# Down projection: the lo part of u and the left sums kept in HBM for the second half of the columns, and seven products for every second pair of k-tiles there

## The chip, the cores and the metric

The kernel runs on one core of one Trainium2 chip. The metric is device time in microseconds (us), from single executions on the chip; lower is better. The engines are TensorE (PE in the profile, PEld for its weight loads), VectorE (DVE), ScalarE (ACT), GpSimd (POOL) and SyncE (SP). SP and POOL issue nearly all transfers here.

## The reference

One decoder layer over 256 positions with a width of 2048: two attentions over one input projection, an output projection, and then the MLP, which alone matters here:

```python
h = _rmsnorm(x, norm_mlp_pre[layer])
u = jnp.square(jax.nn.relu(h @ w_up[layer]))        # (256, 8192)
x = x + _rmsnorm(u @ w_down[layer], norm_mlp_post[layer])
```

All of it is float32. `w_down` is 8192 x 2048, so the down projection contracts over 64 k-tiles of 128 rows.

## The kernel before

**Split operands.** TensorE multiplies in the form fp32r, so each float32 operand x is split into two tiles, hi and lo: ACT writes hi as a rounded copy, and DVE writes lo = x - hi (`split`, L288 to L292). A product of two operands takes three matmuls of 128x128 by 128x512: hi with hi, hi with lo, lo with hi (`three`).

**Weights.** `Weights` is one stream of weight tiles for the whole kernel. A plain tile is loaded by SP into one of five `raw` buffers (L173) and then split into one of eight pairs of `hi` and `lo` buffers. `plan` puts a tile into the stream; `emit` writes its load and split some tiles ahead of the product that needs it. A function listed in `weights.first[i]` is called just before tile i is emitted. Each engine runs its instructions in the order in which they were emitted, so this order is also the order on DVE, ACT, POOL and SP.

**Down projection.** It runs in two halves of 1024 columns (c = 0, then c = 1), each over 32 pairs of k-tiles. `uT[g]` holds u transposed, four k-tiles for each of the 16 groups g; `split_u` makes its hi and lo (`uhi`, `ulo`, two buffers each) one group ahead, in each half anew.

A plain pair costs 2 tiles x 4 output blocks x 3 = 24 matmuls. The pairs in `DOWN_SEVEN` go by Strassen's scheme in Winograd's form instead, with seven block products, 7 x 3 = 21 matmuls. This text calls such a pair a *seven*. It needs work that a plain pair does not:

- its two weight tiles are loaded by POOL into `ab_down`, which has one buffer (`load_two`, L357);
- `sums` in `seven` forms t and u from them in `st_down` with three DVE adds (L343, L347, L348);
- four tiles are split from these: the corner b11 (128x512) and b from `ab_down`, u and t from `st_down`. The next load of the first half of `ab_down` has to wait for the split of b11, and that of the second half for the split of b;
- `down_sums` (`four_sums`, L910 to L912) and `down_split` form the left sums from u and split them into `shi` and `slo`.

`plan_seven` chooses where `sums` with its load is emitted:

```python
at = max(len(weights.specs) - SUMS_AHEAD, after)     # SUMS_AHEAD = 2; after = end of the seven before
for n, f in (*more, (0, sums)):
    weights.first.setdefault(at - n, []).append(f)
```

So `sums` comes two weight tiles before the seven's first tile, but not before the last tile of the seven ahead of it. Half c = 0 has its sevens at pairs 7, 10, 13, ..., 28 (8 of them), half c = 1 at 3, 6, 9, ..., 27 (9 of them). A plain pair has two weight tiles, so two plain pairs, four tiles, lie between two sevens.

**Other work on DVE in the down projection.** `close` combines the extra products (`md`) at the end of each half; `half_evac` adds them to the first half's results and scales these (L1099 to L1103), early in the second half; `x_back` brings the residual x back from HBM late in the second half.

Of the kernel before, what the change touches and what calls it, by code (L numbers as in the profile page):

```python
# [26 lines left out]
P = 128  # L27
# [18 lines left out]
CW = 1024  # L46
# [51 lines left out]
for _i, _n in enumerate(((11, 12), (13,), (14, 15))):  # L98
    UP_STEPS += [("w", _i)] + [("k", k) for k in _n]

DOWN_SEVEN = (range(7, 29, 3), range(3, 28, 3))
GT = FF // 512
DOWN_STEPS = [[s for kp in range(2 * GT)
               for s in ([("w", kp)] if kp in ws else [("k", 2 * kp), ("k", 2 * kp + 1)])] for ws in DOWN_SEVEN]

# [143 lines left out]
def layer(nc, tc, io):  # L249
# [9 lines left out]
    dram = tc.alloc_tile_pool(name="dram", bufs=1, space=bass.MemoryType.DRAM)  # L259
# [28 lines left out]
    def split(hi, lo, src, g=None):  # L288
        if g is not None:
            return split_gain(hi, lo, src, g)  # L290
        nc.scalar.activation(hi, src, AF.Copy)  # L291
        nc.vector.tensor_tensor(out=lo, in0=src, in1=hi.bitcast(F32), op=OP.subtract)  # L292
# [6 lines left out]
    def tok(t, k, b):  # L299
        return t[:, k, b * P:(b + 1) * P]  # L300
# [25 lines left out]
    def up_weight(j, k):  # L326
        return io["w_up"][k * P:(k + 1) * P, j * CW:(j + 1) * CW]

    late = {}
# [36 lines left out]

        return seven(load, lambda: [late["up"].tile([P, CW], F32, tag="T", bufs=2, name=f"{n}{j}_{kp}") for n in "tu"])

    def plan_seven(sums, fs, after, more=()):

        at = max(len(weights.specs) - SUMS_AHEAD, after)
        for n, f in (*more, (0, sums)):
            weights.first.setdefault(at - n, []).append(f)
        return [weights.plan(f) for f in fs], len(weights.specs)

# [15 lines left out]
    def seven_down(c, kp):  # L391
        def load():
            return load_two(dpl["ab"], nc.gpsimd, io["w_down"][2 * kp * P:(2 * kp + 2) * P, c * CW:(c + 1) * CW])

        return seven(load, lambda: [late["st"][:, i * CW:(i + 1) * CW] for i in range(2)])

    dpl, left, wide_d = {}, {}, []
    for c in range(2):
        wide_d.append([])
        for what, k in DOWN_STEPS[c]:  # L400
            if what == "k":
                ts = [weights.plan(down_weight(c, k), 1, CW)]
            else:
                q, parts_q = (lambda c=c, k=k: down_sums(c, k)), (lambda c=c, k=k: down_split(c, k))
                ts, after = plan_seven(*seven_down(c, k), after, ((2, q), (1, parts_q)))
            wide_d[c].append((what, k, ts))

    def in_order(n, apart=(0, 0)):
# [335 lines left out]
    for what, ch in ch_b:  # L744
# [8 lines left out]
        else:  # L753
# [4 lines left out]
            after = [kr_chain, k_chain[pr]] + ([pair_chain[pr - 1]] if pr else [])  # L758
# [87 lines left out]
    for ns in ((0, 1), (2,), (3,)):  # L846
# [4 lines left out]
        for c, b, acc in proj(mixT, [ch_o[n] for n in ns], f"o{ns[0]}", order, heads_done):  # L851
            n = ns[c]
            if not late:
# [8 lines left out]
                                  in_=io["norm_attn_post"].partition_broadcast(P).rearrange("p o d -> p (o d)"))  # L862
# [11 lines left out]
    uT = {}  # L874
# [22 lines left out]
    def split_u(c, g):  # L897
        if (c, g) == (0, 0):
            uh, ul = [wp.tile([P, CW], F32R, tag=w, bufs=W_BUFS, name=f"u{w}0").rearrange("p (k s) -> p k s", k=4)
                      for w in ("hi", "lo")]  # L900
        else:
            uh, ul = [dpl["dp"].tile([P, 4, S], F32R, tag=f"u{w}", bufs=2, name=f"u{w}{c}_{g}") for w in ("hi", "lo")]
        split(uh.rearrange("p k s -> p (k s)"), ul.rearrange("p k s -> p (k s)"), uT[g].rearrange("p k s -> p (k s)"))
        return uh, ul

    def four_sums(q, f):

        tt = nc.vector.tensor_tensor
        fs, qs = [x.rearrange("p (k s) -> p k s", s=P) for x in (f, q)]
        tt(out=qs[:, 0:2], in0=fs[:, 0:2], in1=fs[:, 1:4:2], op=OP.subtract)  # L910
        tt(out=qs[:, 2], in0=qs[:, 0], in1=fs[:, 3], op=OP.add)
        tt(out=qs[:, 3], in0=fs[:, 2], in1=qs[:, 2], op=OP.subtract)  # L912

    def down_sums(c, kp):
        q = late["st"][:, 2 * CW:2 * CW + 512]
        k = 2 * (kp % 2)
        four_sums(q, uT[kp // 2][:, k:k + 2, :].rearrange("p k s -> p (k s)"))
        left[c, kp] = q

    def down_split(c, kp):  # L920
        st = [dpl["dp"].tile([P, 512], F32R, tag=f"s{w}", bufs=2, name=f"s{w}{c}_{kp}") for w in ("hi", "lo")]
        split(*st, left[c, kp])
        left[c, kp] = [[t[:, i * P:(i + 1) * P] for t in st] for i in range(4)]

    sums = []

# [44 lines left out]
    def close(c, m):  # L971

        tt = nc.vector.tensor_tensor
        nc.scalar.activation(c[0], m[1], AF.Copy)
        for out, x, y, op in ((1, m[6], c[0], OP.subtract), (2, m[7], c[1], OP.subtract),
                              (1, m[5], c[1], OP.add), (3, c[1], m[7], OP.subtract)):
            tt(out=c[out], in0=x, in1=y, op=op)
# [7 lines left out]
    for j in range(FF // CW):  # L985
# [9 lines left out]
        for t, b in order:  # L995
            what, k, tiles = steps[t]
# [26 lines left out]
            first, last = k == 0, k == N_SEVEN - 1  # L1023
# [4 lines left out]
            if last:  # L1028
                more = close(closing(j), m)
# [87 lines left out]
    us = {(0, 0): u_next}  # L1117
    for c in range(2):

        for i, (b, n) in enumerate(PARTS):  # L1120
            y[b][2 * c + n] = bank(4 * c + i, f"y{b}{2 * c + n}")
        accs = {(b, n): y[b][2 * c + n] for b, n in PARTS}
        ws = DOWN_SEVEN[c]
        for t, (what, k, tiles) in enumerate(wide_d[c]):
            g = (2 * k if what == "w" else k) // 4
            u = us[c, g]
            if g >= GT - 2 and c:
                break
            if what == "k":
                w = weights.get(tiles[0])  # L1130
                for b, n in PARTS:
                    down_mm(c, u, k, b, n, w, t == 0, t == len(wide_d[c]) - 1)
                    flow.pump()
                weights.free(tiles[0])
            else:
                if k == ws[0]:
                    if not c:
                        flow.finish(*u_last)
                    else:
                        flow.finish(h_evac)  # L1140
                    m = {i: bank(4 * (1 - c) + o, f"md{i}_{c}") for o, i in enumerate((1, 6, 7, 5))}
                blocks = [[tok(u[x], 2 * (k % 2) + kk, bb) for x in range(2)] for kk, bb in ((0, 0), (1, 0), (1, 1))]
                seven_products(tiles, (blocks, left.pop((c, k))), accs, m, k == ws[0], k == ws[-1])
                if k == ws[-1]:
                    more = close([spare(10, i) for i in range(4)] if c else closing("d"), m)
            nxt = (c, g + 1) if g < GT - 1 else (1, 0)
            if nxt not in us:
                us[nxt] = split_u(*nxt)
            if (c, what, k) == (0, "k", 3):
                weights.limit += 1  # L1150
            if (c, what, k) == (0, "k", 36):
                g_half = [late["up"].tile([P, 512], F32, tag="r", bufs=2, name=f"g_half{n}") for n in range(2)]
                for n in range(2):
# [5 lines left out]
        if not c:  # L1159
            h_evac = flow.start(half_evac(more, g_half))  # L1160
# [64 lines left out]
```

## Time and profile before

| | us |
|---|---|
| median of 3 runs (1053.62 to 1054.93) | 1054.91 |
| the profiled execution | 1055.26 |
| its span, from the first to the last instruction | 1053.5 |
| PE busy, 4863 matmuls | 1042.6 |
| DVE busy | 819.8 |
| ACT busy | 622.5 |
| POOL busy | 46.7 |
| groups `y` and `md` (down projection) in the chain that ended last | 27% and 4% of the span |

The granted TensorE clock was 0.997 of full speed over the span. The profile's page gives busy times and, in 40 slices, the busy share of each engine in tenths. Its chain is followed back from the last instruction. The view of waits says which engine waited for whom; the timeline gives single instructions with their start and length; windows give the busy time in a stretch. A wait of an engine off the chain costs nothing by itself. Line numbers are those of the kernel before; in the changed kernel the same lines stand a few further down (L292 is L294, L343 is L345, L357 is L359).

### The profile page before, as it was taken

The page shows a single profiled execution, that of the slowest core. Times are in us where ns is not written, and L with a number is a line of the kernel's source. Part 1 is how long each engine was busy: PE and PEld are TensorE (multiplying, and loading weights), DVE is VectorE, ACT ScalarE, POOL GpSimd, SP SyncE. Part 2 cuts the span into 40 slices and gives each one's busy share as a digit, 9 for nine tenths or more (in the row PEclk, how much of TensorE's full clock was granted, in tenths as well). Part 3 has the DMA queues.
Part 4 walks back from the last instruction along what each step waited for, and adds up shares of the span by engine and source line. Part 5 has one row for each costly group of instructions (what it writes and reads, how often), then busy time and mean ns, then how long its engine had stood idle before and what let it go on. Part 6 is the DMA issues. An engine that isn't in the chain of part 4 may idle for free.

```text
span 1053.5 us, 13402 instructions
## 1 busy us (share of the span) xinstructions
PE 1042.6 (99%) x4863; PEld 869.2 (83%) x4863; DVE 819.8 (78%) x1090; ACT 622.5 (59%) x832; POOL 46.7 (4%) x88
## 2 busy tenths in 40 slices
PE   9999999999999999999999999999999999999996
PEld 6888889888888788888888888888888888888885
DVE  6676536567557679879888888887899988998985
ACT  6584536565545467666665666666566665666661
POOL 0000000000000000010000100000000000000000
PEclk9999999999999999999999999999999999999998
DMA  9975447454447295647656466467466564667732
GB/s 299 355 236 145 144 130 241 143 161 158 141 167 234 79 350 167 222 143 237 197 186 201 160 215 207 148 224 238 162 218 206 195 221 148 224 210 253 262 121 80
DMA packets 74306, 206.26 MB, mean 196 GB/s; under 512 B 6912, under 2 KB 11520, under 8 KB 73856
## 3 DMA queue, kind: packets, MB, share of 16 engines
q1 hardware_dynamic: 63584, 168.06, 49.0%
q0 software_dynamic: 10080, 36.70, 9.7%
q8 instruction: 38, 0.62, 0.2%
q10 hardware_dynamic: 576, 0.64, 0.2%
q14 instruction: 28, 0.23, 0.1%
HBM read 201.18 MB, written 4.19 MB: 195 GB/s over the span
## 4 chain that ended last, share of the span: by engine, by line
PE 97%; DVE 1%; issue 1%; DMA 0%; ACT 0%; POOL 0%; DVEq 0%; POOLq 0%; ACTq 0%
PE y L281 27%; PE acc_u L281 25%; PE acc_o L281 8%; PE m L281 5%; PE md L281 4%; PE acc_qk L281 4%; PE acc_v L281 4%; PE acc_ckv L281 2%; PE acc_ukv L281 2%; PE acc_q L281 2%; PE acc_cq L281 2%; PE acc_k L281 2%; PE acc_uq L281 2%; PE rt L285 1%; PE sc_b L281 1%
## 5 line engine op out<-in xcount | busy, mean ns | idle before, releaser
L292 DVE TENSOR_TENSOR lo<-raw,hi 128x1024 fp32r<-128x1024 f32 (+3 forms) x219 | 249.2, 1153 | 93.8 <-ACT hi L291 93.1
L291 ACT ACTIVATE hi<-raw 128x1024 fp32r<-128x1024 f32 (+3 forms) x219 | 215.9, 1001 | 117.1 <-PE y L281 40.0
L281 PE MATMUL y<-hi,uhi 128*128 128x512 f32 x394 | 153.6, 390 | 0.0
L281 PE MATMUL y<-hi,ulo 128*128 128x512 f32 x394 | 153.3, 389 | 0.0
L281 PE MATMUL y<-lo,uhi 128*128 128x512 f32 x394 | 153.3, 389 | 0.0
L281 PE MATMUL acc_u<-hi,hT_hi 128*128 128x512 f32 x386 | 153.2, 397 | 0.0
L281 PE MATMUL acc_u<-hi,hT_lo 128*128 128x512 f32 x386 | 150.9, 391 | 0.4 <-DVE hT_lo L292 0.4
L281 PE MATMUL acc_u<-lo,hT_hi 128*128 128x512 f32 x386 | 150.6, 390 | 0.0
L296 DVE SCALAR_TENSOR_TENSOR lo<-raw,gcol,hi 128x1024 fp32r<-128x1024 f32 x86 | 107.6, 1278 | 12.5 <-ACT hi L295 12.3
L295 ACT ACTIVATE hi<-raw,gcol 128x1024 fp32r<-128x1024 f32 x86 | 97.9, 1151 | 24.2 <-PE acc_u L281 13.6
L281 PEld LDWEIGHTS y<-hi,uhi 128*128 128x128 f32 x394 | 74.0, 188 | 15.3
L281 PEld LDWEIGHTS y<-lo,uhi 128*128 128x128 f32 x394 | 74.0, 188 | 15.3
L281 PEld LDWEIGHTS y<-hi,ulo 128*128 128x128 f32 x394 | 73.9, 188 | 15.3
L281 PEld LDWEIGHTS acc_u<-hi,hT_lo 128*128 128x128 f32 x386 | 72.4, 188 | 16.2 <-DVE hT_lo L292 0.8
L281 PEld LDWEIGHTS acc_u<-lo,hT_hi 128*128 128x128 f32 x386 | 72.6, 188 | 14.2
L281 PEld LDWEIGHTS acc_u<-hi,hT_hi 128*128 128x128 f32 x386 | 72.6, 188 | 14.0
L281 PE MATMUL acc_o<-hi,mixT_hi 128*128 128x512 f32 x128 | 51.8, 405 | 0.0
L281 PE MATMUL acc_o<-hi,mixT_lo 128*128 128x512 f32 x128 | 50.2, 392 | 0.0
L281 PE MATMUL acc_o<-lo,mixT_hi 128*128 128x512 f32 x128 | 50.0, 390 | 0.0
L291 ACT ACTIVATE hi<-ab 128x512 fp32r<-128x512 f32 (+1 forms) x38 | 32.0, 843 | 30.0 <-PE acc_u L281 23.2
L281 PE MATMUL m<-hi,st 128*128 128x512 f32 x126 | 45.6, 389 | 0.0
L292 DVE TENSOR_TENSOR lo<-st_down,hi 128x1024 fp32r<-128x1024 f32 x34 | 40.9, 1218 | 2.7 <-ACT hi L291 2.7
(309 smaller groups left out, 1947.7 us busy)
## 6 DMA issues: line engine op xcount, KB each, us to landing
raw<-in_w_down SPq DMA_DIRECT2D x94, 512.0 KB, 4.7
raw<-in_w_up SPq DMA_DIRECT2D x86, 512.0 KB, 4.5
raw<-in_w_in SPq DMA_DIRECT2D x55, 512.0 KB, 5.0
ab<-in_w_up POOLq DMA_DIRECT2D x36, 512.0 KB, 4.9
ab_down<-in_w_down POOLq DMA_DIRECT2D x34, 512.0 KB, 6.2
raw<-in_w_out SPq DMA_DIRECT2D x32, 512.0 KB, 4.0
raw<-in_w_in SPq DMA_DIRECT2D x16, 288.0 KB, 2.8
raw<-in_w_ukv SPq DMA_DIRECT2D x8, 512.0 KB, 4.8
```

The lines of the kernel that those rows point to most:

```text
L281: nc.tensor.matmul(out, a, b, start=start, stop=stop)
L285: nc.tensor.transpose(out, a, ident)
L291: nc.scalar.activation(hi, src, AF.Copy)
L292: nc.vector.tensor_tensor(out=lo, in0=src, in1=hi.bitcast(F32), op=OP.subtract)
L295: nc.scalar.activation(hi, src, AF.Copy, scale=g)
L296: nc.vector.scalar_tensor_tensor(out=lo, in0=src, scalar=g, in1=hi.bitcast(F32), op0=OP.mult, op1=OP.subtract)
```

## The change

**Which pairs are sevens.** `DOWN_SEVEN` becomes pairs 7, 11, 13, 17, 19, 23, 25, 29 in the first half (8, as before) and 3, 5, 7, ..., 27 in the second (13 in place of 9). In the second half one plain pair, two weight tiles, lies between two sevens; in the first half distances of two and four pairs alternate.

**What is kept.** The lo part of u of groups 1 to 15 is written to HBM in the first half (`keep_u`, 15 stores of 512 KB on SP) and loaded back in the second (15 loads on POOL) in place of the DVE subtraction; ACT still makes the hi part. The split left sums of the seven pairs that are sevens in both halves (`SHARED`: 7, 11, 13, 17, 19, 23, 25) are stored by `keep_s` (7 stores on SP) and loaded by `down_back` (7 loads on POOL), in place of `four_sums` and their split. The hi and lo of the left sums become one tile, `s`.

The core of the diff:

```diff
-DOWN_SEVEN = (range(7, 29, 3), range(3, 28, 3))
+DOWN_SEVEN = ((7, 11, 13, 17, 19, 23, 25, 29), range(3, 28, 2))
+SHARED = [k for k in DOWN_SEVEN[0] if k in DOWN_SEVEN[1]]
...
+    def down_parts(c, kp):
+        st = dpl["dp"].tile([P, CW], F32R, tag="s", bufs=2, name=f"s{c}_{kp}")
+        return st, [[st[:, w * 512 + i * P:w * 512 + (i + 1) * P] for w in range(2)] for i in range(4)]
...
+    def down_back(c, kp):
+        st, left[c, kp] = down_parts(c, kp)
+        nc.gpsimd.dma_start(out=st.bitcast(F32), in_=skeep[kp])
...
-    def plan_seven(sums, fs, after, more=()):
+    def plan_seven(sums, fs, after, more=(), last=()):
         at = max(len(weights.specs) - SUMS_AHEAD, after)
-        for n, f in (*more, (0, sums)):
+        for n, f in (*more, (0, sums), *((0, f) for f in last)):
             weights.first.setdefault(at - n, []).append(f)
...
+                more = ((), (back,)) if c and k in SHARED else (((2, q), (1, parts_q)),)
+                ts, after = plan_seven(*seven_down(c, k), after, *more)
...
+        u, h, l = [x.rearrange("p k s -> p (k s)") for x in (uT[g], uh, ul)]
+        if c and g:
+            nc.scalar.activation(h, u, AF.Copy)
+            nc.gpsimd.dma_start(out=l.bitcast(F32), in_=ukeep[g])
+        else:
+            split(h, l, u)
...
+    def keep_u(g):
+        ukeep[g] = dram.tile([P, CW], F32, name=f"ukeep{g}")
+        nc.sync.dma_start(out=ukeep[g], in_=us[0, g][1].rearrange("p k s -> p (k s)").bitcast(F32))
+
+    def keep_s(kp):
+        st, skeep[kp] = skeep[kp], dram.tile([P, CW], F32, name=f"skeep{kp}")
+        nc.sync.dma_start(out=skeep[kp], in_=st.bitcast(F32))
...
+                if not c and k in SHARED:
+                    keep_s(k)
             nxt = (c, g + 1) if g < GT - 1 else (1, 0)
             if nxt not in us:
+                if not c and g > 1:
+                    keep_u(g - 1)
                 us[nxt] = split_u(*nxt)
```

**How the order on DVE moves.** Before, in the second half, from the split of b of the seven at pair 9 to the first add for the seven at pair 12 (`raw` rows are plain weight tiles, `uT` rows the left sums and the lo part of u, brackets the semaphores waited for):

```order
L292 TENSOR_TENSOR lo_7955<-ab_down,hi_7954 128x1024 [waits Activation_49]
L292 TENSOR_TENSOR ulo_4_7965<-uT_4464,uhi_4_7964 128x1024 [waits Activation_49]
L292 TENSOR_TENSOR lo_7969<-st_down,hi_7968 128x1024 [waits Activation_49]
L292 TENSOR_TENSOR lo_7985<-st_down,hi_7984 128x1024 [waits Activation_49]
L910 TENSOR_TENSOR st_down<-uT_4831 128x256
L911 TENSOR_TENSOR st_down<-st_down,uT_4831 128x128 [waits DVE_49]
L912 TENSOR_TENSOR st_down<-uT_4831,st_down 128x128 [waits DVE_49]
L292 TENSOR_TENSOR lo_8006<-raw_8003,hi_8005 128x1024 [waits DMAHW2_49,Activation_49]
L292 TENSOR_TENSOR ulo_5_8022<-uT_4485,uhi_5_8021 128x1024 [waits PE_49,Activation_49]
L292 TENSOR_TENSOR slo_12_8026<-st_down,shi_12_8025 128x512 [waits Activation_49]
L292 TENSOR_TENSOR lo_8032<-raw_8029,hi_8031 128x1024 [waits DMAHW3_49,Activation_49]
L343 TENSOR_TENSOR st_down<-ab_down 128x1024 [waits DMASW3_49,DMASW2_49]
```

Twelve rows lie in this stretch: after the split of b come two splits from `st_down`, the work on u and two plain tiles, and the add that reads `ab_down` is last. In the changed kernel, from the first plain tile ahead of the seven at pair 9 to the plain tiles behind it:

```order
L294 TENSOR_TENSOR lo_7967<-raw_7964,hi_7966 128x1024 [waits DMAHW4_49,Activation_49]
L294 TENSOR_TENSOR lo_7989<-raw_7986,hi_7988 128x1024 [waits DMAHW5_49,Activation_49]
L294 TENSOR_TENSOR lo_8005<-ab_down,hi_8004 128x512 [waits Activation_49]
L294 TENSOR_TENSOR lo_8012<-ab_down,hi_8011 128x1024 [waits Activation_49]
L294 TENSOR_TENSOR lo_8022<-st_down,hi_8021 128x1024 [waits Activation_49]
L294 TENSOR_TENSOR lo_8032<-st_down,hi_8031 128x1024 [waits Activation_49]
L345 TENSOR_TENSOR st_down<-ab_down 128x1024 [waits DMASW2_49,DMASW1_49,DVE_49]
L349 TENSOR_TENSOR st_down<-st_down,ab_down 128x512 [waits DVE_49]
L350 TENSOR_TENSOR st_down<-st_down,ab_down 128x512 [waits DVE_49]
L294 TENSOR_TENSOR lo_8051<-raw_8048,hi_8050 128x1024 [waits DMAHW6_49,Activation_49]
```

The add that reads the next `ab_down` now stands right behind the last split of the seven before it, ahead of the two plain tiles, and the rows on u are gone (pair 11 is one of the seven shared ones).

**How the order on POOL moves.** Before, in the second half, POOL issued only the loads of `ab_down`:

```order
L357 DMA ab_down<-in_w_down 128x1024 [waits DMASW4_49,DVE_49]
L357 DMA ab_down<-in_w_down 128x1024 [waits DMASW5_49,DVE_49]
L357 DMA ab_down<-in_w_down 128x1024 [waits DMASW6_49,DVE_49]
L357 DMA ab_down<-in_w_down 128x1024 [waits DMASW7_49,DVE_49]
L357 DMA ab_down<-in_w_down 128x1024 [waits DMASW0_49,DVE_49]
```

In the changed kernel, from the loads for the seven at pair 7 to those for the seven at pair 11:

```order
L359 DMA ab_down<-in_w_down 128x1024 [waits DMASW7_49,DVE_49]
L359 DMA ab_down<-in_w_down 128x1024 [waits DMASW0_49,DVE_49]
L389 DMA s_7_7874<-skeep_6640 128x1024 [waits DMAHW1_49,PE_49]
L929 DMA ulo_3_7895<-ukeep_6658 128x1024 [waits DMASW6_49]
L359 DMA ab_down<-in_w_down 128x1024 [waits DMASW2_49,DVE_49]
L359 DMA ab_down<-in_w_down 128x1024 [waits DMASW3_49,DVE_49]
L929 DMA ulo_4_7983<-ukeep_6741 128x1024 [waits DMASW1_49,PE_49]
L359 DMA ab_down<-in_w_down 128x1024 [waits DMASW6_49,DVE_49]
L359 DMA ab_down<-in_w_down 128x1024 [waits DMASW7_49,DVE_49]
```

The loads of the kept left sums (`s`) and of the lo part of u (`ulo`) stand between the loads of `ab_down`; those that wait for PE wait until it has read the buffer's former contents.

More of the change, by code (lines that the diff above doesn't have):

```diff
@@ L367, in seven_up, with down_sums, down_split @@
         return seven(load, lambda: [late["up"].tile([P, CW], F32, tag="T", bufs=2, name=f"{n}{j}_{kp}") for n in "tu"])
-    def plan_seven(sums, fs, after, more=()):
+    def down_sums(c, kp):
+        q = late["st"][:, 2 * CW:2 * CW + 512]
+        k = 2 * (kp % 2)
+        four_sums(q, uT[kp // 2][:, k:k + 2, :].rearrange("p k s -> p (k s)"))
+        left[c, kp] = q
+    def down_parts(c, kp):
+        st = dpl["dp"].tile([P, CW], F32R, tag="s", bufs=2, name=f"s{c}_{kp}")
+        return st, [[st[:, w * 512 + i * P:w * 512 + (i + 1) * P] for w in range(2)] for i in range(4)]
+    def down_split(c, kp):
+        q = left[c, kp]
+        st, left[c, kp] = down_parts(c, kp)
+        split(st[:, :512], st[:, 512:], q)
+        skeep[kp] = st
+    def down_back(c, kp):
+        st, left[c, kp] = down_parts(c, kp)
+        nc.gpsimd.dma_start(out=st.bitcast(F32), in_=skeep[kp])
+    def plan_seven(sums, fs, after, more=(), last=()):
         at = max(len(weights.specs) - SUMS_AHEAD, after)
-        for n, f in (*more, (0, sums)):
+        for n, f in (*more, (0, sums), *((0, f) for f in last)):
             weights.first.setdefault(at - n, []).append(f)
@@ L395, in seven_down @@
         return seven(load, lambda: [late["st"][:, i * CW:(i + 1) * CW] for i in range(2)])
-    dpl, left, wide_d = {}, {}, []
+    dpl, left, skeep, wide_d = {}, {}, {}, []
     for c in range(2):
@@ L403, in layer @@
             else:
-                q, parts_q = (lambda c=c, k=k: down_sums(c, k)), (lambda c=c, k=k: down_split(c, k))
-                ts, after = plan_seven(*seven_down(c, k), after, ((2, q), (1, parts_q)))
+                q, parts_q, back = [lambda c=c, k=k, f=f: f(c, k) for f in (down_sums, down_split, down_back)]
+                more = ((), (back,)) if c and k in SHARED else (((2, q), (1, parts_q)),)
+                ts, after = plan_seven(*seven_down(c, k), after, *more)
             wide_d[c].append((what, k, ts))
@@ L902, in split_u @@
             uh, ul = [dpl["dp"].tile([P, 4, S], F32R, tag=f"u{w}", bufs=2, name=f"u{w}{c}_{g}") for w in ("hi", "lo")]
-        split(uh.rearrange("p k s -> p (k s)"), ul.rearrange("p k s -> p (k s)"), uT[g].rearrange("p k s -> p (k s)"))
-        return uh, ul
+        u, h, l = [x.rearrange("p k s -> p (k s)") for x in (uT[g], uh, ul)]
[4 more added lines that the diff above has]
+            split(h, l, u)
+        return uh, ul
+    def keep_u(g):
[4 more added lines that the diff above has]
+        nc.sync.dma_start(out=skeep[kp], in_=st.bitcast(F32))
     def four_sums(q, f):
@@ L912, in four_sums @@
         tt(out=qs[:, 3], in0=fs[:, 2], in1=qs[:, 2], op=OP.subtract)
[L914 to L923, printed above, removed]
     sums = []
@@ L1115, in layer @@
     dpl["ab"] = dp.tile([P, 2 * CW], F32, name="ab_down")
-    us = {(0, 0): u_next}
+    us, ukeep = {(0, 0): u_next}, {}
     for c in range(2):
@@ L1159, in layer @@
         if not c:
+            keep_u(GT - 1)
             h_evac = flow.start(half_evac(more, g_half))
```

## The prediction

> **What bounds the kernel now.** I read the busy times first, then TensorE's own waits, then the windows and the chain in the down projection.
>
> ```profile
> PE 1042.6 (99%) x4863; PEld 869.2 (83%) x4863; DVE 819.8 (78%) x1090; ACT 622.5 (59%) x832; POOL 46.7 (4%) x88
> ```
>
> ```profile
> PE warm L476 <- DVE zero L473: 1.2, 1, 1.2
> PE acc_qk L281 <- ACT hi L291: 0.7, 1, 0.7
> PE acc_u L281 <- DVE hT_lo L292: 0.4, 1, 0.4
> PE qrt L285 <- DVE qT L715: 0.2, 1, 0.2
> ```
>
> These four are all of TensorE's waits (us in total, times, longest): 2.5 us, none in the down projection. The kernel is bound by the count of its matmuls. The windows show how near the next engine is, in the second half of the columns:
>
> ```profile
> 720.00:860.00 140.00, 140.00 (x619) 115.91 (x618) 122.34 (x136) 85.89 (x93) 8.64 (x16) 1.00 0.59 200
> 898.00:960.00 62.00, 62.00 (x275) 51.36 (x274) 61.22 (x72) 38.93 (x43) 4.32 (x8) 1.00 0.64 213
> ```
>
> After the length come PE, PEld, DVE, ACT and POOL busy, then the granted clock, the DMA share and GB/s. In the first half (720 to 860) DVE is busy 87% of the time, early in the second 99%, with TensorE still at 100% and the clock at 1.00. The chain gives the pace:
>
> ```profile
> 898.14 10.88 PE y L281 x48
> ...
> 913.78 10.88 PE y L281 x48
> ```
>
> 48 matmuls take 10.88 us, 0.2267 us each. A plain pair (24) is 5.44 us and a seven (21) 4.76 us; two plain pairs and a seven are the 15.64 us from 898.14 to 913.78. After the change one plain pair and one seven repeat: 10.2 us.
>
> **Matmuls removed.** The second half has four more sevens, the first half as many as before: 4 x 3 = 12 matmuls fewer, 12 x 0.2267 = 2.7 us off the path, if TensorE stays the bound.
>
> **The loop through the one buffer ab_down.** These rows show one load from its release to its use (POOL, then DVE):
>
> ```profile
> 903.24 0.54 POOL L357 DMA_DIRECT2D ab_down<-in_w_down  x1 [0.59 <-DVE lo L292]
> ```
>
> ```profile
> 901.12 1.82 DVE L292 TENSOR_TENSOR lo<-ab_down,hi 128x512 fp32r<-128x512 f32 x2
> ...
> 906.27 0.41 DVE L910 TENSOR_TENSOR st_down<-uT 128x256 f32<-128x256 f32 x1
> ...
> 907.26 1.22 DVE L292 TENSOR_TENSOR lo<-raw,hi 128x1024 fp32r<-128x1024 f32 x1
> 908.39 0.68 DVE L292 TENSOR_TENSOR slo<-st_down,shi 128x512 fp32r<-128x512 f32 x1
> 908.99 1.22 DVE L292 TENSOR_TENSOR lo<-raw,hi 128x1024 fp32r<-128x1024 f32 x1
> 910.13 1.22 DVE L343 TENSOR_TENSOR st_down<-ab_down 128x1024 f32<-128x1024 f32 x1
> ...
> 912.72 2.35 DVE L292 TENSOR_TENSOR lo<-raw,hi 128x1024 fp32r<-128x1024 f32 x2
> 914.99 1.82 DVE L292 TENSOR_TENSOR lo<-ab_down,hi 128x512 fp32r<-128x512 f32 x2
> ```
>
> ```profile
> DMA ab_down<-in_w_down: 4.0, 2
> DMA to landing us min/median/max: 4.0/6.2/9.2
> ```
>
> The split of b ends at 902.94 (901.12 + 1.82). POOL issues the second half of the next load 0.3 us later; landing takes a median of 6.2 us from issue. The add waits for it only twice, 4.0 us in all, because 7.2 us of other splits stand between (902.94 to 910.13). In the changed order only u and t stand there (two splits, 1.14 us apart by 907.26 to 908.39: 2.3 us; pairs that aren't shared also have the left sums, 1.0 us by 906.27 to 907.26, and their split, 0.6 by 908.39 to 908.99). The two plain tiles come behind the add. So every seven runs through a closed loop: split of b ends, 0.3 to issue, 6.2 to landing, 0.1 to start, then from the add to the end of the next split of b 910.13 to 916.81, 6.7. That is 13.3 us, against 10.2 us that TensorE takes: 3.1 us short for each seven, whatever else DVE is spared. The left sums lie within the wait.
>
> The same placement exists in the up projection between its second and third seven, and DVE does wait there:
>
> ```profile
> 506.15 1.23 DVE L292 TENSOR_TENSOR lo<-ab,hi 128x1024 fp32r<-128x1024 f32 x1 [1.33 <-ACT hi L291]
> ...
> 511.46 1.22 DVE L343 TENSOR_TENSOR t<-ab 128x1024 f32<-128x1024 f32 x1 [1.82 <-DMA ab<-in_w_up]
> ```
>
> ```profile
> DMA to landing us min/median/max: 3.7/4.9/6.6
> ```
>
> There it is 4.1 us from the split's end (507.38) to the add, and seven plain tiles behind the third seven give the lead back. Here it comes twelve times in a row.
>
> **How much lead there is to eat.** Early in the second half `half_evac` takes DVE's time:
>
> ```profile
> 843.53 1.82 DVE L292 TENSOR_TENSOR lo<-ab_down,hi 128x512 fp32r<-128x512 f32 x2
> ...
> 860.52 2.27 DVE L977 TENSOR_TENSOR c_d<-md,c_d 128x512 f32<-128x512 f32 x3
> ...
> 863.43 1.22 DVE L292 TENSOR_TENSOR ulo<-uT,uhi 128x1024 fp32r<-128x1024 f32 x1
> 864.57 2.35 DVE L292 TENSOR_TENSOR lo<-raw,hi 128x1024 fp32r<-128x1024 f32 x2
> ...
> 876.69 0.69 DVE L292 TENSOR_TENSOR lo<-ab_down,hi 128x512 fp32r<-128x512 f32 x1
> ...
> 892.26 1.22 DVE L292 TENSOR_TENSOR lo<-raw,hi 128x1024 fp32r<-128x1024 f32 x1
> ```
>
> Before, b11 of the seven at pair 3 ends at 877.38 and the first plain tile behind that seven at 893.48, 4.7 us ahead of TensorE (898.14). After the change `close` of the first half waits for pair 29 instead of 28, 5.44 us later (865.96 for 860.52); one `ulo` and two plain tiles (863.43 and the two at 864.57, 3.4 us together) are done ahead of it. So b11 ends at about 879.4, 2.0 later. From there the chain of `half_evac` is as before (16.1 us to that plain tile; the `ulo` in it goes, but ACT's order there still sets the pace), plus the split of the left sums (0.6, and about as much for ACT's part) and the adds for the next seven, 2.6 by 910.13 to 912.72, which now stand ahead of the tile: 879.4 + 16.1 + 1.2 + 2.6 = 899.3. TensorE needs that lo at 898.4 (its second product): it waits 0.9 us. b of pair 5 then ends at 902.2 (two more splits and b11, 2.9). The plain tile behind comes at 902.2 + 6.6 + 2.6 + 1.2 = 912.6; TensorE is ready for it at 898.4 + 0.9 + 10.2 = 909.5. So already the first turn costs its full 3.1 us.
>
> The sevens 3 to 27 have twelve turns; the one from 3 to 5 lies within `half_evac` (the 0.9). Eleven full turns are 11 x 3.1 = 34 us. One of them meets `x_back`:
>
> ```profile
> uT<-xkeep SPq DMA_DIRECT2D x4, 512.0 KB, 7.8
> ```
>
> ```profile
> 970.53 1.23 DVE L343 TENSOR_TENSOR st_down<-ab_down 128x1024 f32<-128x1024 f32 x1 [1.98 <-DMA ab_down<-in_w_down]
> ```
>
> In that stretch the load took the maximum of 9.2 us to land: 3 us more for one turn. At the end DVE has eight plain tiles at 1.14 against 2.72 us on TensorE, and the order to the last output is as before.
>
> **The rest of the change.** *First half:* three turns there have one plain pair as well (11 to 13, 17 to 19, 23 to 25), single ones. In the last seven before, the split of b ended at 845.35 for a product at about 856.4 (18 matmuls, 4.1 us, ahead of the `c_d` at 860.52 that close it), a lead of 11 us; a turn takes 3.1 of it, and the plain tile behind has some 3 us less lead than b, so 5 are left. Then three plain pairs and a seven (21 us on TensorE, about 17 on DVE) give it back: nothing. If landings of 9.2 met all three, some 2 us would show. *The 22 stores on SP:* each is issued right behind a plain load and waits for data long made, so no plain load is held up; the next `ulo` split waits for the store of its buffer's former contents, but only after the split of the tile loaded just ahead, whose own load covers it: nothing. Without that cover a landing like `ab_down`'s, 6.2 less one split of 1.1, would stand on DVE once in a group of 10 us, of which its 13% idle takes 1.4: some 3.5 us a group. *The 22 loads on POOL:* each wait for TensorE there concerns a group or seven read a turn earlier, so it holds no `ab_down` load back. They start about 1 us behind it on the same queue and land, at 6 to 8 us after b, before the plain tile at 10.4: nothing, at most 1 us more landing on each turn (11 us), which I keep for the upper end. *DVE work saved:* 15 `ulo` at 1.14, but four more sevens; a shared turn holds 2.6 + 4 x 1.14 + 0.6 + 1.14 = 8.9 us and one not shared 10.5, a mean of 9.6 under 10.2: DVE alone would not bind, and what is saved becomes waiting.
>
> **Sum.** Against the profiled execution, 1055.26: - 2.7 + 0.9 + 34 + 3 = 1090.5, say 1090 us (the median of the runs is 0.35 lower, which doesn't matter here). Ends: with the up projection's median landing of 4.9 a turn is 12.0, 1.8 short: 1055.3 - 2.7 + 20 + 1 = 1074. With 1 us more landing each turn it is 1102. I take 6.2, since its rows are of this very load beside the same two plain loads.
>
> **Rivals.**
> *Landings as short as the trace has them (A).* Alone on the queues a load lands in 3.7 to 4.0 us; in a loop that waits, the queues may be emptier. A turn is then 11.1 at 4.0, 0.9 short: 1055.3 - 2.7 + 0.9 + 10 = 1063 us. Against it: the two plain loads are still released just ahead of b, as at 902, where it took 6.2. The Trainium skill, "DMA: Bandwidth & Descriptors", section "Anatomy of one DMA — SWDGE (gpsimd) path", fits about 2.0 us plus the bytes at 436 GB/s for such a transfer; an estimate from that page for 512 KB is 3.2 us, by which a turn would be 10.3 and the sum about 1055. No landing of this load in the trace is that short, so the trace disagrees.
> *Faster (B).* The loop never binds and the 2.7 us come through: 1052.5. The point that decides is the time from the end of b to the add: 10.2 - 6.7 = 3.5 us. The shortest landing of all, 3.7 from issue, gives 4.1, so every landing would have to beat the trace, or a lead of 6 us would have to be left after `half_evac` for eleven turns at 0.6 each.
> *More contention (C).* The loads of `ulo` and `s` take turns with `ab_down` on the DMA engines and `x_back` falls on two turns: landings of 7.5 and over, a turn of 14.6 and more: 1055.3 - 2.7 + 11 x 4.4 + 4 = 1105 us and up.
>
> **Chances.** The loop as computed, landings of about 5 to 7 us (1072 to 1102): 0.76. A (1054 to 1071): 0.10. C: 0.08. B: 0.06. The range 1066 to 1104 takes the first case and half of A and leaves about 0.17 out. Two measurements of this kernel are told apart from about 0.2%, 2 us: faster by more only in B, 0.05; within it a part of A and B, 0.03; slower 0.92.
>
> **What would show it.** Waits of DVE (`st_down`) for the load of `ab_down`: some 12 of 3 to 4 us in the second half, about 45 us together, for 2.0 there before. Waits of TensorE (`y`) for DVE's lo, about 3 us once per turn and 38 us in all, the first at the plain tile behind the seven at pair 3 or 5. In the second half from pair 5 on, a turn of 13.3 us on TensorE. No wait of TensorE in the first half. DVE's busy share there falls under 80%. The prediction is wrong if the load lands much sooner in a loop that waits than beside running work, or if `half_evac` leaves DVE well ahead.

## The result, and the profile after

The changed kernel takes 1105.65 us (median of 5 runs, 1104.1 to 1108.57) against 1054.91: a ratio of 1.049 [1.0478, 1.0502]. The profiled execution took 1105.28 us, its span is 1103.5 us, 50.0 more than before's. The prediction had the direction and the loop; its 1090 us were 15 us short, and the time lies just above its range (1066 to 1104).

The busy times, TensorE's waits and DVE's wait for the load, from the page and the chain of waits of the changed kernel (us in total, times, longest):

```profile
PE 1057.1 (96%) x4851; PEld 874.8 (79%) x4851; DVE 815.0 (74%) x1083; ACT 624.8 (57%) x837; POOL 62.7 (6%) x118
```

```profile
PE y L283 <- DVE lo L294: 32.0, 12, 5.3
PE y L283 <- DVE ulo L294: 1.3, 2, 0.6
```

```profile
DVE st_down L345 <- DMA ab_down<-in_w_down: 67.1, 14, 6.9
```

TensorE, which did not wait in the down projection before, waits there 33 us. DVE is not overworked (74% busy): it stands 67 us in fourteen waits for `ab_down`. The same two stretches as in the windows before:

```profile
720.00:860.00 140.00, 136.85 (x595) 112.25 (x594) 116.12 (x131) 80.14 (x88) 8.46 (x16) 0.99 0.75 261
898.00:960.00 62.00, 52.80 (x215) 41.93 (x214) 43.84 (x50) 32.64 (x37) 8.04 (x15) 0.94 0.58 197
```

In the first half (720 to 860) TensorE now loses 3.2 us, which the prediction said would not happen; in the second 9.2 of 62 us, and DVE falls from 99% to 71%. One turn of the second half on DVE, on POOL and at TensorE:

```profile
918.63 1.82 DVE L294 TENSOR_TENSOR lo<-ab_down,hi 128x512 fp32r<-128x512 f32 x2
...
923.14 1.23 DVE L294 TENSOR_TENSOR lo<-st_down,hi 128x1024 fp32r<-128x1024 f32 x1
926.82 1.22 DVE L345 TENSOR_TENSOR st_down<-ab_down 128x1024 f32<-128x1024 f32 x1 [2.46 <-DMA ab_down<-in_w_down]
...
929.42 2.35 DVE L294 TENSOR_TENSOR lo<-raw,hi 128x1024 fp32r<-128x1024 f32 x2
```

```profile
920.74 0.54 POOL L359 DMA_DIRECT2D ab_down<-in_w_down  x1 [0.60 <-DVE lo L294]
```

```profile
917.63 0.50 PE L283 MATMUL y<-lo,uhi 128*128 128x512 f32 x1 [3.21 <-DVE lo L294]
930.69 0.50 PE L283 MATMUL y<-lo,uhi 128*128 128x512 f32 x1 [0.95 <-DVE lo L294]
```

The split of b ends at 920.45, POOL issues 0.3 later, the add starts 6.4 us after the split's end, and TensorE starts the plain tile 0.05 us after its lo is made. Between 917.63 and 930.69 lie 13.06 us, for work that takes 10.2.

The first plain tiles behind the sevens start at 904.0 and, eleven turns later, at 1060.4: a mean turn of 14.22 us. From its first matmul (706 us) to its last, the down projection on TensorE takes 386.3 us, 47.6 more than before (338.7): 2.7 saved, 5.7 lost in the first half, 44.3 in the eleven turns, 0.3 in the tail. Of the 2.4 us that are left of the 50.0, 2.2 lie behind the last instruction of DVE.

### The profile page after: what moved, and what is told of

It reads as the page before. It is cut to its first block, busy times and chain, and to the rows that moved or that the text cites. A ratio compares the mean times of both kernels' runs of the same rounds, so it can differ in the third digit from the quotient of the medians.

```text
span 1103.5 us, 13459 instructions
## 1 busy us (share of the span) xinstructions
PE 1057.1 (96%) x4851; PEld 874.8 (79%) x4851; DVE 815.0 (74%) x1083; ACT 624.8 (57%) x837; POOL 62.7 (6%) x118
## 4 chain that ended last, share of the span: by engine, by line
PE 76%; issue 10%; DMA 9%; DVE 3%; ACT 0%; POOL 0%; SPq 0%; POOLq 0%; DVEq 0%; ACTq 0%
PE acc_u L283 24%; PE y L283 12%; PE acc_o L283 8%; DMA ab_down<-in_w_down 7%; PE m L283 5%; PE acc_qk L283 4%; PE acc_v L283 4%; PE acc_ckv L283 2%; PE acc_ukv L283 2%; PE acc_q L283 2%; PE acc_cq L283 2%; PE acc_k L283 2%; PE acc_uq L283 2%; DVE lo L294 1%; DMA ukeep<-ulo 1%
## 5 line engine op out<-in xcount | busy, mean ns | idle before, releaser
L294 DVE TENSOR_TENSOR lo<-raw,hi 128x1024 fp32r<-128x1024 f32 (+3 forms) x211 | 239.0, 1150 | 88.2 <-ACT hi L293 87.5
L293 ACT ACTIVATE hi<-raw 128x1024 fp32r<-128x1024 f32 (+3 forms) x211 | 206.9, 997 | 72.3 <-DMA raw<-in_w_in 15.1
L283 PE MATMUL y<-lo,uhi 128*128 128x512 f32 x370 | 150.8, 407 | 32.0 <-DVE lo L294 32.0
L283 PE MATMUL y<-hi,ulo 128*128 128x512 f32 x370 | 149.2, 403 | 1.3 <-DVE ulo L294 1.3
L283 PE MATMUL y<-hi,uhi 128*128 128x512 f32 x370 | 149.3, 403 | 0.0
L345 DVE TENSOR_TENSOR st_down<-ab_down 128x1024 f32<-128x1024 f32 x21 | 25.7, 1223 | 67.1 <-DMA ab_down<-in_w_down 67.1
L293 ACT ACTIVATE hi<-ab_down 128x512 fp32r<-128x512 f32 (+1 forms) x42 | 35.2, 841 | 58.7 <-DMA ab_down<-in_w_down 44.6
L293 ACT ACTIVATE hi<-st_down 128x1024 fp32r<-128x1024 f32 x42 | 43.2, 1051 | 27.7 <-DVE st_down L350 20.9
L294 DVE TENSOR_TENSOR lo<-st_down,hi 128x1024 fp32r<-128x1024 f32 x42 | 50.3, 1219 | 2.3 <-ACT hi L293 2.3
```

Source lines behind the costliest of these rows:

```text
L283: nc.tensor.matmul(out, a, b, start=start, stop=stop)
L345: tt(out=two[0], in0=two[1][:, 0:2, :], in1=two[1][:, 1:4:2, :], op=OP.add)
```

## The experiments

The table has all of them. Each ratio is to the kernel before as it was measured along with that run (medians of 1054.61 to 1055.17 us). "down" is the down projection on TensorE, "loads" the number of loads that POOL issues in the whole program, "drain" POOL's last wait before the program ends, read from its sequencer's records. These three are of the profiled execution, which was the fastest for `late_adds` (1069.48 us) and for `both_no_keep` (1069.82).

```
kernel           median us   ratio to before [95%]       down    loads  drain
before           1054.91                                 338.7    70    6.39
changed          1105.65     1.0490 [1.0478, 1.0502]     386.3   100    8.84
late_adds        1074.05     1.0180 [1.0156, 1.0205]     352.5   100    8.84
two_buffers      1060.45     1.0053 [1.0039, 1.0067]     341.2   100    8.84
spacing_only     1103.97     1.0466 [1.0451, 1.0480]     387.6    78    7.04
both             1054.56     0.9998 [0.9989, 1.0007]     336.0   100    8.84
keep_u_only      1055.78     1.0004 [0.9995, 1.0013]     338.9    85    7.61
stores_on_act    1110.54     1.0525 [1.0510, 1.0539]     391.9   100    8.84
both_act         1063.33     1.0075 [1.0062, 1.0088]     348.1    78    7.04
many_loads       1065.13     1.0095 [1.0081, 1.0109]     338.6   100    8.84
many_loads2      1057.24     1.0020 [1.0011, 1.0029]     338.7   100    8.84
both_one_load    1056.36     1.0015 [1.0006, 1.0024]     335.9    67    6.16
both_no_keep     1071.83     1.0156 [1.0141, 1.0170]     354.8    78    7.04
both_short_end   1052.35     0.9975 [0.9965, 0.9985]     336.0    73    6.64
```

### Is it the loop? Later adds, and a second buffer

`late_adds`: the load stays where it is, the three adds move behind the two plain tiles, right ahead of the seven's own first tile.

```
+        if fetch:
+            weights.first.setdefault(len(weights.specs), []).append(sums)
+            sums = fetch      # only the load is issued at the old place
```

> The changed kernel with one order moved: the load of ab_down is issued where it was, but the three adds that read it are emitted right before the seven's own first tile, behind the two plain tiles. Theory (a closed loop through the one buffer): the two plain splits fall into the wait, so a turn of the second half is about 6.9 (end of the split of b to landing, as in the changed kernel) + 0.1 + 2.6 + 0.6 + 1.1 = 11.4 us instead of 13.7 to 14.2; TensorE loses about 1.2 us a turn and some 6 us at x_back, nothing in the first half: 1067 us (1060 to 1075). Rival 1 (DVE simply has too much work): the amount of work is the same, so 1100 to 1106. Rival 2 (the transfers added on POOL and SP fill the DMA engines): the same bytes, so 1100 to 1106.

1074.05 us: 31.6 of the 50.7 us are gone, so the loop accounts for most of the loss. What stays has another wait:

```profile
PE y L283 <- DMA ulo<-ukeep: 10.3, 6, 2.8
```

On POOL the load of the kept lo of u stands behind the load of `ab_down`, which waits for a split of b that now comes later. In the first half TensorE has no wait left (20.00 of 20 us busy in each window from 720 to 880).

`two_buffers`: adds where they were, but every second seven of the second half, from pair 7, loads into `uT[0]`, `uT[1]`, free by then.

```
+            if c and kp % 4 == 3 and kp > 3:
+                two = [uT[i].rearrange("p k s -> p (k s)") for i in range(2)]
```

> The changed kernel with a second buffer for the weights of every other seven of the second half (the tiles of u of groups 0 and 1, which nobody reads any more by then); the adds stay where they were. Theory (closed loop): the load is released a whole turn earlier and no longer waits for the split of b just ahead, so turns fall to 10.2 to 10.6 us; the 5.8 us lost in the first half stay: 1060 us (1055 to 1068). Rival 1 (too much work on DVE): 1095 to 1106. Rival 2 (DMA engines full): 1090 to 1106.

1060.45 us; DVE's waits for `ab_down` fall from 67.1 us to three, all in the first half, and TensorE does not stop between 898 and 960:

```profile
DVE st_down L345 <- DMA ab_down<-in_w_down: 15.2, 3, 5.4
```

```profile
898.00:960.00 62.00, 62.00 (x275) 51.20 (x274) 60.47 (x71) 43.79 (x50) 11.74 (x22) 1.00 0.79 282
```

The one buffer is shown as the cause of the 44 us.

`both` has the two edits together.

> The changed kernel with both edits: adds behind the two plain tiles in both halves, and the second buffer in the second half. Theory (closed loop): no turn is longer than TensorE's 10.2 us, and in the first half a turn costs 3 us of a lead of about 8; the 12 matmuls saved come through: 1053 us (1051 to 1058), a ratio of about 0.998. Rival 1 (too much work on DVE): over 1090. Rival 2 (DMA engines full, x_back above all): 1065 to 1090.

1054.56 us: the down projection is at 336.0, the 2.7 us of twelve matmuls shorter than before's, and yet the time does not move. What the matmuls saved was lost behind them. The last instructions of DVE, of the kernel before and of `both`:

```profile
1048.04 1.54 DVE L1072 SCALAR_TENSOR_TENSOR uT<-uT,rstd_fin,uT 128x512 f32<-128x512 f32 x3
```

```profile
1045.74 1.54 DVE L1107 SCALAR_TENSOR_TENSOR uT<-uT,rstd_fin,uT 128x512 f32<-128x512 f32 x3
```

They end at 1049.58 and 1047.28; the spans at 1053.5 and 1053.4. So 3.9 us follow in the one and 6.1 in the other.

### What keeping in HBM is worth

`spacing_only`: the new spacing of the sevens, nothing kept.

```
-SHARED = [k for k in DOWN_SEVEN[0] if k in DOWN_SEVEN[1]]
+SHARED = []
-        if c and g:
+        if False:
```

> The new spacing of the sevens alone: nothing is kept in HBM, the lo of u and all left sums are made on DVE in the second half too. Theory (closed loop): the left sums fall into the wait, one split of u per turn stands between the two plain tiles, on the loop, so a turn is 6.5 + 0.1 + 6.7 + 1.1 = 14.4 us; without the 22 stores the first half loses nothing: 1100 us (1092 to 1108). Theory on the stores: in the first half the loads of ab_down behind a close seven land about 6.5 us after the split of b instead of 8.7 to 9.2, and TensorE doesn't wait there. Rival 1 (too much work on DVE): 25 us more of DVE work make it slower by as much, 1125 us. Rival 2 (DMA engines full): 22 MB less to move, so well under 1090.

1103.97 us: about as slow as the changed kernel, so the spacing makes the loss. TensorE's waits in this run, then the landings of `ab_down` from 890 to 1075 us, first of this run, then of the changed kernel:

```profile
PE y L283 <- DVE lo L294: 21.8, 13, 4.1
PE y L283 <- DVE ulo L294: 6.6, 12, 0.6
```

```profile
DMA to landing us min/median/max: 5.4/5.8/9.8
```

```profile
DMA to landing us min/median/max: 4.3/6.6/10.1
```

Without the 22 loads a landing is 0.8 us shorter; but the split of u (1.14 us) stands in the turn again, so a turn is no shorter (mean 14.65). In the first half TensorE has no wait, and the three tight landings are 5.4 us after the split of b; in the changed kernel they are 9.07, 8.66 and 9.15.

`keep_u_only`: the other way round, the old spacing with lo of u kept (15 stores, 15 loads; no left sums are shared at that spacing).

> Old spacing of the sevens (every third pair in both halves), but lo of u is kept in HBM and loaded back (15 stores on SP, 15 loads on POOL; no pair is a seven in both halves, so no left sums are kept). Theory (with this spacing a load that lands 2 to 3 us late is still early enough, so the stores that hold up SP cost nothing; what is left is the end of the program: POOL's last drain took 6.39, 7.04 and 8.84 us with 70, 78 and 100 loads issued on POOL, 0.0817 us for each load, so 85 loads give 7.6 us, 1.2 more than before, of which 0.2 is covered by SP): 1055.6 us (1054.8 to 1057), ratio 1.001, no TensorE wait of 1 us or more in the down projection. Rival 1 (the stores on SP stall TensorE at this spacing too): 1058 to 1062, with TensorE waits for lo in the first half. Rival 2 (DVE work saved is worth time by itself): below 1054.

1055.78 us: no change that can be told, as forecast, with one more us behind the last landing. DVE is spared a fifth of its work in the second half (61.22 us of 62 before), and nothing is gained where TensorE is the bound:

```profile
898.00:960.00 62.00, 62.00 (x275) 51.39 (x274) 48.82 (x58) 38.17 (x42) 7.50 (x14) 1.00 0.76 257
```

`both_no_keep` is `both` with the edit of `spacing_only`.

> The kernel 'both' with nothing kept in HBM (lo of u and the left sums are made anew in the second half, as in spacing_only). Theory (keeping is worth nothing as long as the loop of load and adds sets the turn, but with the loop broken DVE is at 19.3 to 19.9 us of 20 between 900 and 1000 us, and making lo of u anew adds 1.2 us to each turn and the sums 1.6 us to seven of them): DVE becomes the bound in the second half, TensorE waits for lo there, 1062 us (1056 to 1070). Rival (DVE has lead enough from the stretches around it): 1053 (1052 to 1054.5), keeping is worth nothing at all; POOL's drain is 7.0 us in either case.

1071.83 us, beyond my range, by the mechanism forecast: DVE is full, ten turns lie between the adds at 896.33 and 1012.58, 11.62 us each, against 10.2 that TensorE takes. Here DVE is the bound:

```profile
898.00:960.00 62.00, 59.73 (x248) 45.22 (x248) 61.32 (x81) 35.93 (x42) 6.45 (x12) 1.00 0.55 179
```

So keeping is worth some 17 us with the loop broken (1071.83 against 1054.56), nothing in the changed kernel and nothing at the old spacing.

### The first half: stores that hold up SP

In the changed kernel SP waits for the split of u before it may store it (720 to 885 us), and the plain loads stand behind. The third tight turn on SP, DVE and TensorE:

```profile
SPq L936 <- DVE ulo L294: 21.5, 4, 6.2
```

```profile
817.27 0.45 SPq L175 DMA_DIRECT2D raw<-in_w_down  x1
823.87 0.32 SPq L936 DMA_DIRECT2D ukeep<-ulo  x1
824.28 1.67 SPq L175 DMA_DIRECT2D raw<-in_w_down  x2
```

```profile
822.63 1.22 DVE L294 TENSOR_TENSOR ulo<-uT,uhi 128x1024 fp32r<-128x1024 f32 x1
...
834.25 1.22 DVE L345 TENSOR_TENSOR st_down<-ab_down 128x1024 f32<-128x1024 f32 x1 [5.41 <-DMA ab_down<-in_w_down]
```

```profile
825.27 0.54 POOL L359 DMA_DIRECT2D ab_down<-in_w_down  x1 [1.73 <-DVE lo L294]
```

```profile
838.11 0.50 PE L283 MATMUL y<-lo,uhi 128*128 128x512 f32 x1 [1.88 <-DVE lo L294]
```

The split ends at 823.85 and SP stores at 823.87: no data "long made". The store, two plain loads and both halves of `ab_down` all go out between 823.00 and 825.95, and `ab_down` lands 9.15 us after the split of b.

`stores_on_act` puts the 22 stores on ACT's queue.

```
-        nc.sync.dma_start(out=ukeep[g], ...
+        nc.scalar.dma_start(out=ukeep[g], ...
```

> The changed kernel with its 22 stores (lo of u, left sums) issued on ACT's queue instead of SP's; nothing else differs. Theory (the first half's 5.8 us come from the stores that wait on SP for the split of u and hold up the loads behind them, so that the tight turns' ab_down lands together with them): 1100 us (1097.5 to 1102), the tight turns' landings 6 to 7 us after the split of b instead of 8.7 to 9.2, TensorE without a wait until the second half; second half as before. Rival 1 (it is the stores' bytes that slow the loads, whichever queue issues them): 1104.5 or more and landings still over 8 us. Rival 2 (ACT now waits for DVE's split of u, and the hi copies behind it come late): 1103 or more, with ACT waits for ulo.

1110.54 us. The half of the theory that speaks of landings held: 4.96, 5.64 and 6.39 us in the tight turns. So it is the stores on SP that made them late in the changed kernel; `spacing_only`, without the stores, agrees. The time did not follow, and rival 2 is not the reason, for ACT has no wait for `ulo`. ACT issues the store late in its own order, and the next split of u, which writes over the same buffer, waits for the store to land:

```profile
DVE ulo L294 <- DMA ukeep<-ulo: 18.3, 8, 3.2
```

```profile
778.36 1.23 DVE L294 TENSOR_TENSOR ulo<-uT,uhi 128x1024 fp32r<-128x1024 f32 x1 [2.23 <-DMA ukeep<-ulo]
```

This is the wait that the prediction priced as "without that cover", in milder form. With two buffers for lo of u the store has to go out in a narrow stretch of time: early, it blocks SP; late, it blocks DVE. A third buffer wasn't tried.

`both_act` puts the stores and the 22 loads on ACT's queue in `both`.

> The kernel 'both' (adds late, second buffer) with the 22 stores and the 22 loads of what was kept issued on ACT's queue, so that POOL issues 78 loads instead of 100. Theory ('both' saved 2.3 us at TensorE's last matmul and lost 2.2 of it in POOL's last drain, 8.84 us for 100 loads against 6.39 for 70): the drain takes 7.0 us, so 0.4 of the 2.2 stays and the time is 1052.8 us (1051.8 to 1053.8), ratio 0.998. Rival 1 (the end does not depend on POOL's loads): 1054.6, ratio 1.000. Rival 2 (ACT's order is held up by a store or a load that waits, and hi copies come late): 1055 or more, with TensorE waits.

1063.33 us: the time of rival 2. The drain is 7.04 us as forecast, but TensorE waits again, for the lo of u and not for hi copies as that rival had it:

```profile
PE y L283 <- DMA ulo<-ukeep: 4.8, 2, 2.6
PE y L283 <- DVE ulo L294: 3.0, 2, 2.4
```

### The 2.2 us behind the last instruction

POOL's last wait began in every kernel 0.6 us before its last arithmetic instruction (for `rstd_fin`) ended. It lasted 6.39, 6.16, 6.64, 7.04, 7.61 or 8.84 us with 70, 67, 73, 78, 85 or 100 loads: 0.0817 us for each load issued on POOL in the whole program. `many_loads` is the kernel before with 30 small loads on POOL, at about 208 us.

```
+        for i in range(30):
+            nc.gpsimd.dma_start(out=idle[:, i * 8:i * 8 + 8], in_=io["gains"][:, 0:8])
```

> The kernel before with 30 small loads (128x8 f32, 4 KB each, never read) added on POOL's queue at about 208 us, where POOL has nothing to do for 110 us: 100 POOL loads instead of 70. Theory (POOL's last drain grows by 0.0817 us for each load it issued, whatever its size and however early): drain 8.84 us, time 2.2 us over before: 1056.8 (1056.2 to 1057.4), ratio 1.002. Rival 1 (the drain goes by bytes, or by loads of the last stage): 1054.6 within 0.5. Rival 2 (the small loads disturb the loads of that stage): over 1058, with TensorE waits between 208 and 240 us.

1065.13 us, more than the theory gives, though the drain is 8.84 us. Its new tile of 960 bytes had moved other tiles in SBUF, and TensorE was slower from the start, long before the loads. `many_loads2` sends 30 loads of 128x3 to a tile that the kernel had as padding.

> many_loads with its 30 small loads (128x3 f32, never read) going to a tile that the kernel before already has as padding, so that no other tile moves in SBUF. Theory (the 30 loads cost only POOL's last drain, 8.84 instead of 6.39 us; the other 7.6 us of many_loads, spread over stages before and after the loads, came from its new tile of 960 bytes that moved all others): 1057.3 (1056.7 to 1057.9), ratio 1.002, TensorE's last matmul where it was, at 1045 us. Rival (the small loads themselves slow the kernel): 1060 or more.

1057.24 us, as forecast: the down projection is as before, and loads of 1.5 KB cost the drain as much as loads of 512 KB. Shown.

`both_one_load` issues the two loads of a pair of tiles as one.

```
-        for i in range(2):
-            queue.dma_start(out=raw[:, i * CW:(i + 1) * CW], ...
+        queue.dma_start(out=raw.rearrange("p (i n) -> p i n", i=2), ...
```

> The kernel 'both' with the two loads of 128x1024 that fill ab or ab_down issued as one load of 128x2x1024 (18 in the up stage, 15 here): POOL issues 67 loads instead of 100, of the same bytes. Theory ('both' saved 2.3 us at TensorE's last matmul, and POOL's last drain, 0.0817 us for each load issued, took 2.2 of it): drain 6.1 us, the end as short as before's, 1052.6 us (1051.6 to 1053.6), ratio 0.998. Rival 1 (the drain goes by rows or bytes and not by loads): drain 8.8, 1054.6, ratio 1.000. Rival 2 (one load of 1 MB lands later than two of 512 KB, and the adds wait): TensorE waits in the down projection, 1055 or more.

The drain is 6.16 us and the end short, but 1056.36: the up projection lost 3.6 us, where TensorE now waits for DVE:

```profile
PE acc_u L283 <- DVE c L1011: 2.0, 2, 1.3
```

`both_short_end` takes the one load in the down projection alone, and puts the loads into the second buffer on SP.

> The kernel 'both' with the up stage's loads two by two as before (both_one_load lost 3.5 us there), the down projection's two loads into ab_down as one, and the loads into the second buffer on SP's queue: POOL issues 73 loads instead of 100. Theory (what 'both' saves at TensorE, 2.3 us, is lost only in POOL's last drain): drain 6.6 us, ending with SP's own last wait as before's does, 1052.8 us (1051.8 to 1053.9) if before is at 1055.1, ratio 0.998. Rival 1 (SP is held up by the loads into the second buffer, which wait until it is free, and raw loads behind them come late): TensorE waits in the second half, 1056 or more. Rival 2 (the end does not follow the drain): ratio 1.000.

1052.35 us, ratio 0.9975 [0.9965, 0.9985]: faster than the changed kernel, and by a quarter of a per cent than the kernel before. TensorE's last matmul ends at 1042.0 (before: 1045.0) and the span at 1050.5. SP now waits 64.9 us to load into the second buffer, and TensorE has no wait in the down projection:

```profile
SPq L422 <- DVE lo L294: 64.9, 8, 14.5
```

## Where the prediction was right, and why it was wrong

The mechanism was right: a closed loop through the one buffer, in which DVE waits for the load and TensorE for DVE. The sum was 15 us short in four terms. The step that failed most is "waits for data long made, so no plain load is held up", by which the first half cost nothing: it cost 5.7 us. The landing in the loop (nearly 4 us), the turns at `x_back` (3.4 us) and the end of the program (2.2 us) make up the rest.

- *Matmuls removed, - 2.7 us*: right. With the loop gone the down projection is 2.7 us shorter.
- *The loop, 11 x 3.1 = 34 us*: right in kind, and shown by `late_adds` and `two_buffers`; the landing was too small. From the split of b to landing I took 0.3 + 6.2 = 6.5 us; nine turns had a median of 6.9. The 22 loads that I priced at nothing lie beside `ab_down`; in `spacing_only`, without them, the same turns had 6.1. That is 9 x 0.4, nearly 4 us.
- *`x_back`, one turn at 9.2, + 3 us*: mis-sized, and its cause misread. Two turns were slow, with 9.04 and 10.36 us from the split of b to landing, 15.85 and 17.17 us long; against 13.3 that is 6.4 us, 3.4 more than the term. SP in the changed kernel:

```profile
987.65 0.90 SPq L1116 DMA_DIRECT2D uT<-in_norm_mlp_post  x2
1002.36 2.00 SPq L1107 DMA_DIRECT2D uT<-xkeep  x4
```

  The first slow load, issued on POOL at 989.28 and landed at 998.03, lies beside the two loads of gains and was in before `x_back` issued anything. Only the second, issued at 1005.13 and landed at 1015.20, lies beside `x_back`. In the kernel before, too, the landing of 9.2 us began (961.26) behind the gains:

```profile
959.63 0.90 SPq L1091 DMA_DIRECT2D uT<-in_norm_mlp_post  x2
966.88 2.27 SPq L1082 DMA_DIRECT2D uT<-xkeep  x4
```

  So most of the 9.2 goes with the gains (9.04 beside them before `x_back` issued), and the turn that meets `x_back` had no term. No run moved either of them, so this rests on the times alone.
- *`half_evac`, 0.9 us*: not seen as a stall of its own. TensorE came 5.8 us later to that place, and the lo there was ready 0.12 us ahead of it.
- *First half: nothing*: wrong, 5.7 us. I had placed the store in the program's order and not in SP's time: SP, up to five raw tiles ahead of DVE, reaches it before the split is done. I had kept "some 2 us" for three landings of 9.2; they came (8.66 to 9.15), and the second and third cost 5.7, part of it by the clock.
- *The end of the program*: no term at all, 2.2 us.
- *DVE work saved "becomes waiting"*: right for the changed kernel (DVE 71% from 898 to 960). The count of DVE's work was right too: 10.5 us for a turn that is not shared, and with the split of u (1.14) that `both_no_keep` makes again 11.6, where 11.62 was measured. So "DVE alone would not bind" holds with keeping only.
- Rival A is excluded (no landing in the turns under 6.2 us after the split of b), and so is B. The time is that of C, by luck: its landings of 7.5 and over came in the two slow turns only, only one of these is `x_back`'s, and 5.7 us came from the first half, which C left at nothing.

## What to carry to other kernels

When a spacing brings two users of one buffer next to each other, add up the whole way round (release, issue, landing, use, release) and compare it with the bound engine's time; a second buffer or a later use then gives back what no saving of work on the waiting engine does. A store on a queue that also feeds loads is placed by when its data is made in time, on that queue's own clock, and its buffer must outlive its landing. After a saving at the bound engine, look at what follows its last instruction before believing that it will show.

## What the runs showed of the hardware that was not expected

- POOL's last wait at the program's end grows by 0.0817 us for each load issued on POOL, whatever its size and however early (67 to 100 loads, 6.16 to 8.84 us). With 70 loads SP's own last wait ended 0.2 us after POOL's and covered it.
- Waits of TensorE can cost more than their length. The granted clock is the third column from the end. From 836.20 to 839.61 us TensorE was busy for 0.90 of 3.41 us (the wait of 1.88 us before 838.11 and one of 0.63); then the clock was 0.50 for 3.41 us, a loss of about 1.7 us, and over the eight microseconds from 838 to 846 it was 0.79:

```profile
836.20:839.61 3.41, 0.90 (x4) 0.51 (x4) 3.38 (x4) 2.57 (x3) 0.00 (x0) 1.00 0.11 32
839.61:843.02 3.41, 3.41 (x10) 2.65 (x9) 3.41 (x4) 2.27 (x3) 1.08 (x2) 0.50 0.75 227
```

```profile
838.00:846.00 8.00, 7.25 (x24) 5.61 (x25) 8.00 (x9) 4.95 (x6) 1.08 (x2) 0.79 0.65 207
```

  The Trainium skill, "TensorE: Matmul & The Clock Gate", section "Part 1: The HAM clock gate (the "warmup" mystery)", says that the clock drops to half after an idle window of about 3.4 us. The trace agrees on the half (0.50 for 3.41 us), but here no single gap was longer than 1.9 us. In the second half TensorE waits for a lo in each of the eleven turns, 0.9 to 5.4 us, so the loop sets the pace and the lower clock costs nothing there.
- A shift of tiles in SBUF by 960 bytes (`many_loads`) made matmuls of 128x512 slower at a clock of 1.00: 405 to 410 ns and 389 to 394 ns, 7.6 us over the kernel. `many_loads2`, with as many loads and no shift, has 405 again. Which tiles matter was not separated.

```profile
L281 PE MATMUL acc_o<-hi,mixT_hi 128*128 128x512 f32 x128 | 51.8, 405 | 0.0
```

```profile
L281 PE MATMUL acc_o<-hi,mixT_hi 128*128 128x512 f32 x128 | 52.5, 410 | 0.0
```

  The first row is of the kernel before, the second of `many_loads`; 389 and 394 ns are the matmuls of `acc_v`.
